# A two-layer diffusion backbone on one core: modulation units moved from the attention to the keys and values, output projection columns tied to residual adds, opening reordered

## The chip, the cores and the metric

The kernel runs on one core of a Trainium2 chip. Five engines work on their own instruction streams, each strictly in the order in which its instructions stand: PE (matrix products), DVE (vector), ACT (activations and copies), POOL and SP; SP issues the DMAs of this kernel. The metric is device time in microseconds (us); lower is better. Three runs of the kernel before took 1841.46, 1844.3 and 1845.71 us, median 1844.3.

## The reference

Two layers act on 512 latent tokens (x) and 256 context tokens (ctx) of width 1024. Layer 0 is windowed grouped-query attention with a sink, layer 1 is retention; each is followed by a SwiGLU FFN. In front of and behind each stands a modulation, whose six parts come from a product of the activated condition with `ada_w`:

```python
for i in range(DEPTH):
    mx = jnp.split(c_act @ ada_w[i] + ada_b[i], 6, axis=-1)
    mc = jnp.split(cc_act @ ada_w[i] + ada_b[i], 6, axis=-1)
    h_x = modulate(rms_norm(x, norm1_g[i]), mx[0], mx[1])
    h_c = modulate(rms_norm(y_ctx, norm1_g[i]), mc[0], mc[1])
    ...
    x = x + mx[2] * out_x
    x = x + mx[5] * swiglu(modulate(rms_norm(x, norm2_g[i]), mx[3], mx[4]), ffn_w_in[i], ffn_w_out[i])
    ...
```

Parts 0 and 1 are needed before the first key can be computed, part 2 at the residual add behind the attention, parts 3 and 4 at the first FFN, part 5 behind it.

## The kernel before

**Number format.** Weights and hidden tiles are split into a high and a low half: `whi` is a copy rounded on ACT (L137 or L162, 128x1024), `wlo` the difference on DVE (L138 or L163). A product is three matmuls: whi with the high hidden half, wlo with the high one, whi with the low one (`mm3`, L142; `keys` and `values` do the same with lines of their own, L392 and L403).

**The opening** (up to `St.close()`) loads x, the first two parts of `ada_w` as four quarters (`adaQ`, 4 x 512 KB each), the key and value weights, the context, rotary tables and masks, all issued by SP in program order. `stats0`, `ada_quarter`, `hidden0`, `keys` and `values` stand in a hand-written order for PE, DVE and ACT (`manual_schedule`). `ada_quarter(q)` makes the modulation of 2 of 8 hidden tiles: 32 products of 32 condition columns on PE (64 instructions), `rows` copied by ACT, two transposes on PE, then on DVE three small operations for the latent stream (s = 0) and three for the context (s = 1). `hidden0(s, k...)` then makes the scaled tile `hs` on DVE, the high half of `h` on ACT and the low half on DVE. `keys(s, q)` and `values(s, q)` use the hidden tiles 2q and 2q + 1. `split_w` splits the next of four key and value weights. The DMA tiles of quarters and of two of these weights share the tag `adan` with 8 buffers.

**The attention** follows: 24 blocks (4 head groups x 4 latent and 2 context blocks) whose instructions a scheduler interleaves. A block scores four heads on PE (L614), takes the minimum with mask and sink on DVE (L615), exponentials on ACT, the scaling on POOL (L628), transposes on PE (L637), copies, and value products on PE (L649). The query projections (`make_q`) of the next group stand between the blocks of the first three groups. After blocks 14, 16, 18 and 20 `ada_unit` makes four more pieces of modulation, units 4, 5 (part 2), 8 (part 4, tiles 0 to 3) and 6 (part 3, tiles 0 to 3): each loads four 512 KB tiles through the two `wraw` buffers that the weight stream uses, 32 products on PE (64 instructions, L286), a copy, one transpose (L291), two small DVE operations.

**The output projection** works on eight output tiles d in two batches of four weights: for each batch first the latent stream, then the context. Each tile is 24 matmuls into one of two `pj` banks, `gated_add` on DVE (L241) adds it to the residual and frees the bank, `add_square` collects the norm. The remaining columns of parts 3 and 4 (tiles 4 to 7 of each, eight in all) are made on DVE by `ada_tile` (L258, two instructions of 128x1024 a tile), one behind each of the first eight adds of the loop, and nothing but the scheduler sets where they stand on DVE.

## Time and profile before

The profiled execution took 1842.23 us, of which the span of its instructions is 1840.4 us.

| what | value |
|---|---|
| busy share of the span | PE 97%, weight loads 83%, DVE 61%, ACT 37%, POOL 7% |
| chain of work that ended last | PE 85%, DVE 6%, ACT 3%, DMA 2%, POOL 2% |
| granted TensorE clock, mean of the span | 0.995 |
| HBM read | 174.29 MB, 96 GB/s over the span |
| opening, up to the last value product | 0 to 83 us |
| attention | 85 to 326 us |
| output projection | 326 to 390 us |

Busy time of PE is the union of matmuls whose ends are modelled, so a busy PE may still be short of its peak rate: consecutive 128x512 matmuls start 0.23 us apart at full clock though each is listed with 0.39 us. A row of the timeline shows start, length, engine, line, operation, tiles and, in brackets, how long the engine sat idle before it and what released it.

### The profile page before, as it was taken

The numbers are of one execution on the slowest core, as the hardware profiler recorded it, in microseconds if no ns is written. First come the engines' busy times: TensorE is split into PE (matmuls) and PEld (weight loads), VectorE is DVE, ScalarE is ACT, GpSimd is POOL, SyncE is SP. The second block draws the span as 40 slices with busy tenths as digits, with TensorE's granted clock in tenths as the row PEclk, the third lists the DMA queues.
The fourth block names the chain that finished last, engine by engine and source line by source line (L and its number), as shares of the span: only waits on it lengthen the run. The fifth ranks groups of instructions, "written<-read, shape, count | busy, mean of one in ns | idle before, by whom it ended". The sixth has DMA issues, their size and how long they took to land.

```text
span 1840.4 us, 26468 instructions
## 1 busy us (share of the span) xinstructions
PE 1787.8 (97%) x10718; PEld 1534.0 (83%) x10718; DVE 1126.5 (61%) x2005; ACT 688.1 (37%) x1198; POOL 126.3 (7%) x228
## 2 busy tenths in 40 slices
PE   5999999999999999999999999999999989999999
PEld 4877766788888888888888888888888889999998
DVE  6787676768544545363675553553552698777774
ACT  5676666343221212121252322322421364445442
POOL 0044433000000000000011000010010000000000
PEclk9999999999999999999999999999999999999999
DMA  8100035535332425162521230220220333333232
GB/s 339 52 27 12 1 103 185 172 103 161 103 99 86 123 71 170 50 218 78 172 71 46 69 92 24 80 81 24 92 74 19 92 105 92 102 115 115 78 95 80
DMA packets 50955, 178.11 MB, mean 97 GB/s; under 512 B 5648, under 2 KB 6032, under 8 KB 50576
## 3 DMA queue, kind: packets, MB, share of 16 engines
q1 hardware_dynamic: 50832, 176.41, 30.6%
q8 instruction: 84, 1.38, 0.3%
q14 instruction: 39, 0.32, 0.1%
HBM read 174.29 MB, written 2.10 MB: 96 GB/s over the span
## 4 chain that ended last, share of the span: by engine, by line
PE 85%; DVE 6%; ACT 3%; DMA 2%; POOL 2%; issue 1%; SPq 0%; DVEq 0%; POOLq 0%; ACTq 0%
PE pj L146 10%; PE pj L145 10%; PE pj L147 10%; PE Y L811 6%; PE gu L145 4%; PE gu L146 4%; PE gu L147 4%; PE Z L811 3%; PE guc L147 2%; PE guc L145 2%; PE guc L146 2%; PE pv L145 2%; PE pv L147 2%; PE pv L146 2%; PE pv L1032 2%; PE pv L1033 2%
## 5 line engine op out<-in xcount | busy, mean ns | idle before, releaser
L137 ACT CAST whi<-wraw 128x1024 fp32r<-128x1024 f32 x174 | 182.3, 1049 | 261.1 <-PE pj L147 147.0
L138 DVE TENSOR_TENSOR wlo<-wraw,whi 128x1024 fp32r<-128x1024 f32 x174 | 215.4, 1239 | 82.1 <-ACT whi L137 81.1
L146 PE MATMUL pj<-h,wlo 128*128 128x512 f32 (+1 forms) x512 | 181.9, 355 | 4.4 <-DVE wlo L138 4.3
L145 PE MATMUL pj<-h,whi 128*128 128x512 f32 (+1 forms) x512 | 184.2, 360 | 1.7 <-DVE res L241 1.0
L147 PE MATMUL pj<-h,whi 128*128 128x512 f32 (+1 forms) x512 | 180.5, 354 | 0.2 <-DVE h L231 0.2
L241 DVE SCALAR_TENSOR_TENSOR res<-pj,mod,res 128x512 f32<-128x512 f32 (+1 forms) x160 | 104.7, 656 | 113.3 <-PE pj L147 112.8
L258 DVE CUSTOM_DVE_ANT_0 junk<-adaw,crow_sb,small_sb 128x1024 bf16<-128x1024 f32 x96 | 123.1, 1282 | 36.8 <-DMA adaw<-in_adaT_dram 34.4
L145 PE MATMUL pj<-ax,whi 128*128 128x512 f32 x352 | 138.3, 393 | 0.0
L146 PE MATMUL pj<-ax,wlo 128*128 128x512 f32 x352 | 137.5, 391 | 0.0
L145 PE MATMUL gu<-h,whi 128*128 128x512 f32 x352 | 137.4, 390 | 0.0
L146 PE MATMUL gu<-h,wlo 128*128 128x512 f32 x352 | 137.3, 390 | 0.0
L147 PE MATMUL pj<-ax,whi 128*128 128x512 f32 x352 | 137.1, 389 | 0.0
L147 PE MATMUL gu<-h,whi 128*128 128x512 f32 x352 | 136.9, 389 | 0.0
L146 PEld LDWEIGHTS pj<-h,wlo 128*128 128x128 f32 x512 | 97.6, 191 | 17.1 <-DVE wlo L138 5.3
L145 PEld LDWEIGHTS pj<-h,whi 128*128 128x128 f32 x512 | 97.4, 190 | 16.0 <-issue 1.5
L147 PEld LDWEIGHTS pj<-h,whi 128*128 128x128 f32 x512 | 97.4, 190 | 13.4 <-issue 0.8
L147 PE MATMUL guc<-h,whi 128*128 128x256 f32 x352 | 99.7, 283 | 0.0
L146 PE MATMUL guc<-h,wlo 128*128 128x256 f32 x352 | 99.6, 283 | 0.0
L145 PE MATMUL guc<-h,whi 128*128 128x256 f32 x352 | 99.6, 283 | 0.0
L162 ACT CAST whi<-wraw 128x1024 fp32r<-128x1024 f32 x59 | 61.7, 1053 | 76.9 <-PE pj L147 34.9
L106 ACT ACTIVATE hn<-gu 128x512 f32<-128x512 f32 x22 | 13.2, 598 | 197.4 <-PE gu L147 197.4
L163 DVE TENSOR_TENSOR res<-pv,res 128x512 fp32r<-128x512 f32 x24 | 16.6, 692 | 114.0 <-ACT res L162 114.0
(307 smaller groups left out, 4361.3 us busy)
## 6 DMA issues: line engine op xcount, KB each, us to landing
wraw<-in_wst_dram SPq DMA_DIRECT2D x214, 512.0 KB, 3.6
adaw<-in_adaT_dram SPq DMA_DIRECT2D x64, 512.0 KB, 4.2
adan<-in_adaQ_dram SPq DMA_DIRECT2D x16, 512.0 KB, 7.7
wraw<-in_adaN_dram SPq DMA_DIRECT2D x16, 512.0 KB, 4.3
res<-in_xT_dram SPq DMA_DIRECT2D x16, 256.0 KB, 5.2
res<-in_cT_dram SPq DMA_DIRECT2D x8, 256.0 KB, 6.3
crow_sb<-in_crow_dram SPq DMA_DIRECT2D x2, 1024.0 KB, 5.1
out_dram<-res SPq DMA_DIRECT2D x8, 256.0 KB, 2.0
```

Source lines behind the costliest of these rows:

```text
L137: nc.scalar.copy(hi, raw)
L138: nc.vector.tensor_tensor(lo, raw, hi, op=sub)
L145: nc.tensor.matmul(o, whi, xhi, start=first, stop=False)
L146: nc.tensor.matmul(o, wlo, xhi, start=False, stop=False)
L147: return nc.tensor.matmul(o, whi, xlo, start=False, stop=last)
L162: nc.scalar.copy(hi, t)
L163: return nc.vector.tensor_tensor(lo, t, hi, op=sub)
L241: nc.vector.scalar_tensor_tensor(res[d], o, mods[l, s][:, part, d:d + 1], res[d], mult, add)
L258: after(nc.vector.tensor_tensor_reduce(junk, w, cr[:, s * 1024:(s + 1) * 1024], 1.0, sm_t[:, C_ADAB + l * 48 + j:C_ADAB + l * 48 + j + 1], ...
L811: nc.tensor.matmul(o, p, r, start=first and k + i == 0, stop=k == 3 and i == 2, skip_group_check=not first)
L1032: nc.tensor.matmul(vo, hi[:, tok], wk_[1][:, cs], start=False, stop=False)
L1033: nc.tensor.matmul(vo, lo[:, tok], wk_[0][:, cs], start=False, stop=k == KT - 1)
```

## The change

The four units leave the attention. Their 16 loads are issued by SP right behind the masks, through the 8 `adan` buffers, after the load of the first query weight (`q0_raw`), which is issued early too; every later weight load stands behind them on SP. Their products, copies and transposes are written into the opening's manual order, between `keys` and `values`; the fourth one's transpose stands behind `values(0, 2)`.

In the opening, work is put between the products of a quarter and its transposes (`fill`): two dummy matmuls (`busy`, whose result is overwritten) in quarter 0, halves of `values` or `keys` in the others. Only the three DVE operations of the latent stream stand ahead of its hidden tiles; those of the context are handed back as a function (`c1`) and come later. The low half of a weight (`split_low`) is separated from the high half (`split_w`), and the fourth weight's high half is made earlier. `keys` runs each of its three products over both hidden tiles before the next. The first `values(0, 2)` matmul is held behind the last `keys` matmul.

In the output projection `WO_ADA` names the adds that an `ada_tile` follows: (0, 0) to (0, 6) and (1, 2), that is five in the first batch and three in the second; each now must stand behind its add on DVE (an order without a semaphore).

```diff
-UNITS_AT = (14, 16, 18, 20)
 UNITS = (4, 5, 8, 6)
+WO_ADA = [(0, d) for d in range(7)] + [(1, 2)]
...
+    def unit_load(u):
+        w = []
+        for kk in range(4):
+            w.append(T(st_p, 1024, "adan", 8))
+            nc.sync.dma_start(w[kk], adaN[u, kk])
+        return w
+
+    def ada_unit(u, w):
         part, d0 = u // 2, u % 2 * 4
-        o = pj()[:, 0:P]
+        o = pT()[:, 0:P]
         for kk in range(4):
-            w = T(rp, 1024, "wraw", 2)
-            nc.sync.dma_start(w, adaN[u, kk])
...
         rows = T(cp, 256, "rows", 2)[:, 0:P]
         nc.scalar.copy(rows, o)
+        def finish():
...
+        return finish
...
-    def ada_quarter(q, w):
+    def ada_quarter(q, w, fill):
...
         nc.scalar.copy(rows, o)
+        fill()
         t = pT()[:, 0:256]
...
+        columns(0)
+        return lambda: columns(1)
...
+    q0_raw = w_raw()
+    wu = [unit_load(u) for u in UNITS]
...
+    def busy(n):
+        nc.tensor.matmul(kvv[2][:, :n], ones, res0[0][0][:, :n], start=True, stop=True)
...
         stats0(0)
         split_w(st_p)
-        ada_quarter(0, wq[0])
-        hidden0(0, 0, 1)
+        c1 = ada_quarter(0, wq[0], lambda: busy(256))
+        busy(SX)
+        hidden0(0, 0, 1, between=(split_low,))
+        c1()
         split_w(st_p)
+        split_low()
         keys(0, 0)
         split_w(rp)
+        split_low()
         squares0(1)
-        ada_quarter(1, wq[1])
+        c1 = ada_quarter(1, wq[1], lambda: values(0, 0, (0, 1)))
         hidden0(0, 2, 3)
-        values(0, 0)
+        c1()
+        values(0, 0, (2, 3))
         rms(1, bank=pT)
         keys(0, 1)
-        ada_quarter(2, wq[2])
+        c1 = ada_quarter(2, wq[2], lambda: values(0, 1, (0, 1)))
+        c1()
         hidden0(1, 0, 1)
+        split_w(rp)
         hidden0(1, 2, 3)
         hidden0(0, 4, 5)
-        split_w(rp)
-        values(0, 1)
-        ada_quarter(3, wq[3])
+        values(0, 1, (2, 3))
+        c1 = ada_quarter(3, wq[3], lambda: keys(1, 0))
+        c1()
+        split_low()
         hidden0(1, 4, 5)
-        keys(1, 0)
         keys(1, 1)
         hidden0(0, 6, 7)
+        c1 = ada_unit(UNITS[0], wu[0])
         keys(0, 2)
         hidden0(1, 6, 7)
+        c1()
+        c1 = ada_unit(UNITS[1], wu[1])
         values(1, 0)
         values(1, 1)
+        c1()
...
+        c1 = ada_unit(UNITS[2], wu[2])
         keys(1, 2)
+        c1()
         keys(0, 3)
-        keys(1, 3)
+        last_key = keys(1, 3)
+        c1 = ada_unit(UNITS[3], wu[3])
...
-        values(0, 2)
+        after(values(0, 2), [last_key])
+        c1()
...
-            if 6 * g + i in UNITS_AT:
-                ada_unit(UNITS[UNITS_AT.index(6 * g + i)])
...
-                gated_add(s, 0, 2, d, o, res)
+                ins = gated_add(s, 0, 2, d, o, res)
                 add_square(s, d, res[d])
-                if ada_wo and (s or d < 4):
-                    ada_tile(0, *ada_wo.pop(0), (0, 1), cr, wo_p, 4)
+                if (s, d) in WO_ADA:
+                    ada_tile(0, *ada_wo.pop(0), (0, 1), cr, wo_p, 4, [ins])
```

More of the change, by code (lines that the diff above doesn't have):

```diff
@@ L131, in w_parts, with next_w @@
         return T(pool, 1024, "whi", bufs, F32R), T(pool, 1024, "wlo", bufs, F32R)
-    def next_w(pool, own=2):
-        raw = w_raw()
+    def next_w(pool, own=2, raw=None):
+        raw = raw or w_raw()
         hi, lo = w_parts(pool, own)
@@ L240, in gated_add @@
     def gated_add(s, l, part, d, o, res):
-        nc.vector.scalar_tensor_tensor(res[d], o, mods[l, s][:, part, d:d + 1], res[d], mult, add)
+        return nc.vector.scalar_tensor_tensor(res[d], o, mods[l, s][:, part, d:d + 1], res[d], mult, add)
     def cond_rows(pool):
@@ L272, in dit_kernel @@
     ln_exp_turn()
-    def ada_unit(u):
+    def unit_load(u):
[5 more added lines that the diff above has]
+    def ada_unit(u, w):
         part, d0 = u // 2, u % 2 * 4
-        o = pj()[:, 0:P]
+        o = pT()[:, 0:P]
         for kk in range(4):
-            w = T(rp, 1024, "wraw", 2)
-            nc.sync.dma_start(w, adaN[u, kk])
             for a in range(2):
@@ L285, in ada_unit @@
                     c0 = a * 512 + j * P
-                    nc.tensor.matmul(o[32 * j:32 * j + 32, :], ccol[:, 2 * kk + a, :], w[:, c0:c0 + P],
+                    nc.tensor.matmul(o[32 * j:32 * j + 32, :], ccol[:, 2 * kk + a, :], w[kk][:, c0:c0 + P],
                                      start=kk + a == 0, stop=kk + a == 4)
@@ L289, in ada_unit @@
         nc.scalar.copy(rows, o)
-        t = pj()[:, 0:P]
-        nc.tensor.transpose(t, rows, ident)
-        tv = t.rearrange("p (j c) -> p c j", c=32)
-        for s in range(2):
-            nc.vector.tensor_tensor(mods[0, s][:, part, d0:d0 + 4], tv[:, s, :],
-                                    sm_t[:, C_ADAB + 4 * u:C_ADAB + 4 * u + 4], op=add)
+        def finish():
+            t = pT()[:, 0:P]
+            nc.tensor.transpose(t, rows, ident)
+            tv = t.rearrange("p (j c) -> p c j", c=32)
+            for s in range(2):
+                nc.vector.tensor_tensor(mods[0, s][:, part, d0:d0 + 4], tv[:, s, :],
+                                        sm_t[:, C_ADAB + 4 * u:C_ADAB + 4 * u + 4], op=add)
+        return finish
     def ada_quarter_load(q):
@@ L320, in ada_quarter, with columns @@
         bias = sm_t[:, C_ADAB:C_ADAB + 16].rearrange("p (f d) -> p f d", f=2)[:, :, 2 * q:2 * q + 2]
-        for s in range(2):
+        def columns(s):
             col = mods[0, s][:, 0:2, 2 * q:2 * q + 2]
@@ L341, in split_w, with split_low @@
     def split_w(pool):
-        w = raw[len(wkv)]
         wkv.append((T(pool, 1024, "whi", 2, F32R), T(pool, 1024, "wlo", 2, F32R)))
-        split(w, *wkv[-1])
+        nc.scalar.copy(wkv[-1][0], raw[len(wkv) - 1])
+    def split_low():
+        i = lows.pop(0)
+        nc.vector.tensor_tensor(wkv[i][1], raw[i], wkv[i][0], op=sub)
+    lows = [0, 1, 2, 3]
     wkv = []
@@ L373, in stats0, with hidden0 @@
         rms(s, bank=pT)
-    def hidden0(s, *ks):
+    def hidden0(s, *ks, between=()):
         y, ts = ssq[s], []
@@ L381, in hidden0 @@
             nc.scalar.activation(h[s][k][0], ts[-1], AF.Identity, bias=mods[0, s][:, 0, k:k + 1])
+        for b in between:
+            b()
         for k, t in zip(ks, ts):
@@ L387, in keys, with values @@
             o = kvx[j] if s == 0 else kvc[:, j * SC:(j + 1) * SC]
-            for k in (2 * q, 2 * q + 1):
-                ws = slice(k * P, (k + 1) * P)
-                (whi, wlo), (xhi, xlo) = wkv[j], h[s][k]
-                for i, (a, b) in enumerate(((whi, xhi), (wlo, xhi), (whi, xlo))):
-                    nc.tensor.matmul(o, a[:, ws], b, start=k + i == 0 and (s == 0 or j == 0),
-                                     stop=k == KT - 1 and i == 2, skip_group_check=s == 1)
-    def values(s, q):
-        for t in ((0, 1, 2, 3), (4, 5))[s]:
+            for i, (a, b) in enumerate(((0, 0), (1, 0), (0, 1))):
+                for k in (2 * q, 2 * q + 1):
+                    last = nc.tensor.matmul(o, wkv[j][a][:, k * P:(k + 1) * P], h[s][k][b],
+                                            start=k + i == 0 and (s == 0 or j == 0),
+                                            stop=k == KT - 1 and i == 2, skip_group_check=s == 1)
+        return last
+    def values(s, q, tiles=None):
+        first = None
+        for t in tiles or ((0, 1, 2, 3), (4, 5))[s]:
             tok = slice((t - 4 * s) * P, (t - 4 * s) * P + P)
@@ L402, in values @@
                 for i, (a, b) in enumerate(((hi, whi), (hi, wlo), (lo, whi))):
-                    nc.tensor.matmul(o, a[:, tok], b[:, cs], start=k + i == 0 and t % 2 == 0,
-                                     stop=k == KT - 1 and i == 2, skip_group_check=True)
+                    ins = nc.tensor.matmul(o, a[:, tok], b[:, cs], start=k + i == 0 and t % 2 == 0,
+                                           stop=k == KT - 1 and i == 2, skip_group_check=True)
+                    first = first or ins
+        return first
     with tc.manual_schedule(engines={mybir.EngineType.PE, mybir.EngineType.DVE, mybir.EngineType.Activation}):
@@ L478, in dit_kernel, with make_q @@
     q, stats = {}, {}
-    def make_q(j):
-        w = next_w(ap, 1)
+    def make_q(j, raw=None):
+        w = next_w(ap, 1, raw)
         qs = T(ap, 36, "qs", 4).rearrange("p (f n) -> p f n", f=3)
@@ L547, in dit_kernel @@
     wsel[0] = 2
-    q0 = make_q(0)
+    q0 = make_q(0, q0_raw)
     with tc.manual_schedule(engines={mybir.EngineType.PE}):
-        values(0, 2)
+        after(values(0, 2), [last_key])
+        c1()
         rope_key(kn[0])
```

## The prediction

> **What bounds the kernel now.** I read the chain of waits first, then windows of the three touched stages, then the timeline where PE waits.

> ```profile
> PE 85%; DVE 6%; ACT 3%; DMA 2%; POOL 2%; issue 1%; SPq 0%; DVEq 0%; POOLq 0%; ACTq 0%
> ```

> PE sets the end: what shortens PE's list or a wait on it counts, work elsewhere only where PE waits for it. The windows give PE, weight loads, DVE, ACT and POOL busy, the granted clock, DMA share and GB/s:

> ```profile
> 10.00:20.00 10.00, 6.05 (x68) 3.61 (x68) 7.90 (x27) 5.10 (x8) 0.00 (x0) 1.00 1.03 420
> ...
> 18.77:22.18 3.41, 0.44 (x2) 0.20 (x2) 3.27 (x9) 1.01 (x2) 0.00 (x0) 1.00 1.02 419
> 22.18:25.60 3.42, 3.28 (x8) 2.47 (x9) 3.12 (x4) 2.63 (x4) 0.00 (x0) 0.50 1.03 407
> 42.66:46.07 3.41, 1.60 (x60) 1.33 (x52) 3.10 (x7) 2.00 (x4) 0.00 (x0) 1.00 1.01 354
> ...
> 353.27:356.69 3.42, 0.90 (x4) 0.30 (x2) 3.42 (x7) 0.42 (x1) 0.00 (x0) 1.00 0.00 0
> 356.69:360.10 3.41, 1.65 (x4) 1.36 (x5) 3.41 (x6) 0.00 (x0) 0.00 (x0) 0.50 0.24 29
> ```

> The early opening is short of DMA and DVE, not of PE. 420 GB/s makes 1.25 us for each 512 KB tile. After a 3.4 us stretch with PE 0.44 or 0.90 us busy, the clock was 0.50 in the next; after 1.60 us it was not.

> ```profile
> 46.27 1.03 ACT L162 CAST whi<-adan 128x1024 fp32r<-128x1024 f32 x1
> 47.21 0.36 ACT L315 COPY rows<-pT 128x256 f32<-128x256 f32 x1
> ...
> 47.35 0.39 PE L403 MATMUL kvv<-whi,h 128*128 128x256 f32 x1 [3.09 <-ACT whi L162]
> 47.62 0.44 PE L318 MATMUL pT<-const_sb,rows 128*128 128x128 f32 x2
> ```

> The first matmul of values(0, 2) had slipped ahead of the last quarter's transposes and held PE 3.09 us; but the `rows` copy which these need ended at 47.57 anyway.

> ```profile
> 355.97 1.28 DVE L258 CUSTOM_DVE_ANT_0 junk<-adaw,crow_sb,small_sb 128x1024 bf16<-128x1024 f32 x1
> 357.17 1.22 DVE L138 TENSOR_TENSOR wlo<-wraw,whi 128x1024 fp32r<-128x1024 f32 x1
> ...
> 354.66 0.47 PE L145 MATMUL pj<-h,whi 128*128 128x512 f32 x1 [0.96 <-DVE res L241]
> 358.45 0.79 PE L146 MATMUL pj<-h,wlo 128*128 128x512 f32 x1 [3.31 <-DVE wlo L138]
> ```

> In the output projection DVE works through modulation columns, so the second batch's first low half is late: PE waits 0.96 and 3.31 us, then starts about a dozen matmuls 0.43 us apart instead of 0.23.

> **Part 1, the opening: +7.9 us.** A unit is 64 PE instructions; 64 of the same shape took 1.95 us at 42.31 (L312). Four, with four transposes of some 0.05 to 0.2 us, make 8.0 us. What the new order gives back I walked step by step from the rows of before.
> - *Quarter 0.* Dropping three of the six DVE column operations (19.83 to 20.77) brings the hidden tiles 0.5 us forward; but both low weight halves (1.23 us each) now stand behind them on DVE, and keys(0, 0) needs them: it ends near 27.0 instead of 26.8. The dummy matmuls (about 0.45 and 0.9 us) fill an idle stretch; they save the eight slow matmuls (0.2 each), but keys(0, 0) then waits for DVE instead. Taken: 0; bounds -1.6 (all eight) and +0.9 (dummies in the way).
> - *Quarter 1.* Half of values(0, 0) runs in the 1.46 us that PE waited for `rows`; keys(0, 1) still waits for its hidden tiles, whose DVE start at 31.6 does not move (seven context squares stand ahead). It ends near 36.3 instead of 36.55.
> - *Quarter 2.* The fill is 12 matmuls 0.12 apart, 1.45 us, but `rows` was ready at 39.02: the transposes move from 39.07 to about 39.45, and DVE's chain (columns, context, tiles 4 and 5) 0.4 us later with them.
> - *Quarter 3.* PE loses the 3.09 us wait, but `rows` still stands on ACT behind the high halves of tiles 4 and 5, ready about 47.25. keys(1, 0), 1.45 us, is done in the wait. Together PE is 1.9 us ahead at 47.6.
> - *The units' weights.* Behind the masks (44.96 in before, near 44.5 now) land the query weight and 16 tiles, 1.25 us apart: the units are complete at 50.9, 55.8, 60.7 and 65.6. PE is there at 49.1, 54.5, 59.4 and 67.0: the first costs 0.5 us of waiting, the others nearly nothing, since tiles are used as they land. The second unit's last tile takes the fourth weight's buffer, freed by its low half at 49.9, in time. Each reuse of the eight buffers also waits for PE, 4 to 9 us before PE needs the tile.
> - *Behind.* values(0, 2) ends at 71.9 instead of 64.78. ACT reaches the key copies only after the fourth unit's `rows` (68.8), the query's high half stands behind six of them (3.4 us), its low half behind the rotary steps on DVE: 74.9, where it was 67.0. That wait, 1.02 us in before, comes back whole.
> Later weight loads stand behind the 16 on SP; the next lands near 66.9 and is needed near 89. So 74.9 - 67.0 = +7.9. Bounds: +1 (all waits named above, 3.1 + 1.5 + 0.7 + 1.6 us, are gone) and +12 (two half-clock stretches of 1.7 us and DMA 1 us late at two units).

> **Part 2, the attention: -10.8 us.** The 256 unit matmuls (L286) are 12.9 us of busy PE there, more than 8.0, as each run of a few is cut into by scores. Are they additive, or do they fill gaps? Blocks 6 to 11 ended 55.2 us after block 5, with 16.6 us of query projection (two tiles of 24 matmuls 0.228 us apart and 24 matmuls 0.118 apart) and 2.4 of norms: 36.2 for the blocks. Blocks 18 to 23 took 48.4 with 6.4 of units and 5.8 of output projection: 36.2 again. So filler adds. But with the units gone, blocks 19 to 21 stand almost bare in the new PE order, and PE waited 0.5 to 0.7 us several times there for DVE, POOL and ACT; I give back 2.1 us. Bounds: -4 (only the waits for unit tiles and switching) and -13.8.

> **Part 3, the output projection: -3.9 us.** Five columns instead of eight in the first batch free 3 x 2.9 us of DVE (two of 1.28 and their accumulator reads each) ahead of the second batch's low halves. The first is then done near 351, before PE asks. Gone: 0.96 + 3.31 us and 12 x 0.2 us of half clock, with the pauses between, 7.1 us. The three later tiles cost nothing: DVE needs 2.9 + 0.75 + 0.69 = 4.3 us beside 5.5 us of PE per output tile; without that cover each would cost 2.9. But the scheduler now puts 23 more of its matmuls (5.2 us) into the attention; the first batch, DVE-bound until 350 (DVE 9.8 of 10 busy from 335 to 355), takes only about 2 us of that, the rest becomes a wait for banks: +3.2. Bounds: -7.1 and -1.

> [...]

> **Sum.** +7.9 - 10.8 - 3.9 = -6.8 us on the profiled execution, 1842.23 us (span 1840.4): 1835.4. That run lies 2.07 below the median 1844.3, so the forecast is 1837.5; its own range, from half of each part's bounds, 1832 to 1842.

> **Rivals.**
> - *The opening gains what its waits show* (3.1, 1.5, 0.7 and the slow matmuls, 6.9 in all): for it, these rows are idle PE; against it, ACT and DVE end the next wait each time. 1837.5 - 6.9 = 1830.6.
> - *Units were cover in the attention*: for it, blocks 18 to 23 hold many short waits for DVE and POOL; against it, the equal 36.2. -4 in place of -10.8, but then the early output matmuls cost nothing either (-3.2): 1841.
> - *Slower: the unit loads are late.* The eight tiles of the last two units reuse buffers that PE frees. If they come at the pace of the attention's unit loads, 4.3 us from issue to landing, one after the other, the last lands at 55.8 + 8 x 4.3 = 90 instead of 65.6, and PE, in order, stands 23 us at 67: 1860. For it: SP waits in order for each buffer. Against it: four buffers come free at once. It decides from about 3 us a tile (55.8 + 8 x 3.1 - 67 = 14 us, twice the forecast's gain).
> - *The tie does nothing*: the low halves stay behind the columns. Against it: in the new DVE order the first stands behind the add of (1, 1), ahead of four column instructions. Without part 3: 1841.4.

> **Chances.** A difference of 0.2% (3.7 us) is about what runs of this kernel can tell. Forecast 0.54, opening gains 0.13, cover 0.15, slower 0.13, tie 0.05. Faster by over 0.2% (below 1840.6): 0.13, the forecast's own lower part 0.48, a share of the middle cases 0.09: 0.70. Within: 0.16. Slower: 0.14. The range 1828 to 1847 leaves out the late loads and little else.

> **What would show it.** The opening: values(0, 2) ending near 72 us, the first query product near 75, unit waits below 1 us. The attention: no unit line, last value product near 326. The output projection: no wait over 1 us for a low half, no 0.50 clock there. Wrong if PE waits several us for unit tiles, or blocks 18 to 23 take over 45 us.

## The result and the profile after

| | median | runs | ratio to the kernel before |
|---|---|---|---|
| before | 1844.54 us | 4 (1841.46 to 1845.71) | |
| after | 1832.42 us | 4 (1831.61 to 1833.5) | 0.9937, 95% interval 0.992 to 0.9954 |

The profiled execution of the changed kernel took 1832.84 us, its span 1831.05. The forecast was 1837.5; the time lies 5.1 below it, near the lower end of the range of 1832 to 1842.

The chain of waits of the changed kernel has the same owner as before:

```profile
PE 86%; DVE 5%; ACT 2%; DMA 2%; POOL 2%; issue 1%; SPq 0%; POOLq 0%; ACTq 0%; DVEq 0%
```

So the time can be counted along PE. I cut both spans at three PE instructions: the second product of the first query (the first that needs its low half), the attention's last value product, and the first product of the FFN.

| stretch of the span | before | after | difference |
|---|---|---|---|
| opening, to the query's second product | 67.04 | 76.95 | +9.91 |
| attention, to its last value product | 258.18 | 248.14 | -10.04 |
| output projection, to the first FFN product | 70.02 | 62.71 | -7.31 |
| rest | 1445.2 | 1443.25 | -1.95 |

23 more matmuls of the output projection stand ahead of the last value product than before, 0.228 us each, 5.2 us in all. For like work (these 23 counted in the same stretch both times) the attention gave 15.3 us and the output projection 2.1.

Not all of these stretches repeat equally well from profile to profile. The opening of the changed kernel stands unchanged in five profiles, its own included, and took 75.62 to 77.27 us in them; the opening of before took 67.04 and 68.67 us in two. So a difference of up to 1.65 us there can be chance. The attention repeats within 0.1 us where the clock is the same: 248.1 to 248.2 us in three profiles with full clock in it.

The opening, in the timeline of the changed kernel (start, length, engine, line, operation, tiles, idle time before it and its releaser):

```profile
46.19 1.38 ACT L406 ACTIVATE h<-hs,mod 128x512 fp32r<-128x512 f32 x2 [1.21 <-DVE hs L405]
47.48 0.35 ACT L324 COPY rows<-pT 128x256 f32<-128x256 f32 x1
...
47.89 0.44 PE L328 MATMUL pT<-const_sb,rows 128*128 128x128 f32 x2 [2.21 <-ACT rows L324]
51.39 0.64 PE L291 MATMUL pT<-adan,ccol 128*32 128x128 f32 x16 [0.58 <-DMA adan<-in_adaN_dram]
52.62 0.65 PE L291 MATMUL pT<-adan,ccol 128*32 128x128 f32 x16 [0.58 <-DMA adan<-in_adaN_dram]
...
75.69 0.49 PE L145 MATMUL pj<-h,whi 128*128 128x512 f32 x1 [0.54 <-ACT whi L137]
76.95 0.50 PE L146 MATMUL pj<-h,wlo 128*128 128x512 f32 x1 [0.76 <-DVE wlo L138]
```

The last quarter's transposes still wait for `rows`, which ACT makes only behind the high halves of tiles 4 and 5. The 3.09 us stall of a slipped value product is replaced by this one of 2.21. The first unit waits twice for its tiles; the other three run through in 1.88 us each, from one start to the next. Both halves of the query's weight are waited for.

The waits of PE inside the attention (what waited, for what, us in total, times, longest); the first fence is before, the second after:

```profile
PE pT L637 <- POOL pr L628: 5.4, 10, 1.1
PE S L614 <- DVE stat L615: 2.2, 4, 0.7
PE pT L637 <- ACT tt L639: 1.5, 3, 0.7
PE pj L286 <- DMA wraw<-in_adaN_dram: 1.0, 3, 0.4
```

```profile
PE pT L682 <- POOL pr L673: 8.2, 14, 1.1
PE pT L682 <- ACT tt L684: 1.3, 4, 0.4
```

All rows of this view add up to 11.9 us before and 12.6 after. Two kinds have to be taken out for a comparison: the wait for the query's low half, which ends where the stretch begins (1.0 and 0.8), and the units' own tiles (1.0 before). What is left, PE's waits for POOL, DVE and ACT, is 9.9 us before and 11.8 after.

The same stretch by groups of six blocks, each cut at the end of its last value product (PE's waits of 0.15 us and more, in us; unit matmuls in the group; "more" are query and output products that the group holds after and not before; the first group's waits hold the query's):

| blocks | before | waits | unit matmuls | after | waits | more | difference for like work |
|---|---|---|---|---|---|---|---|
| 0 to 5 | 90.4 | 2.7 | 0 | 90.3 | 2.4 | 0 | 0.0 |
| 6 to 11 | 55.3 | 2.3 | 0 | 55.6 | 2.4 | 4 | -0.6 |
| 12 to 17 | 64.6 | 5.1 | 134 | 55.9 | 3.7 | 9 | -10.7 |
| 18 to 23 | 48.4 | 1.8 | 122 | 46.7 | 4.0 | 9 | -3.7 |

The units' instructions, with their transposes and from start to start, took 7.0 us of blocks 12 to 17 and 5.8 us of blocks 18 to 23. So in the one group their leaving gave more than they took, in the other less.

The output projection, in the timeline of the changed kernel, is:

```profile
325.66 1.05 ACT L137 CAST whi<-wraw 128x1024 fp32r<-128x1024 f32 x1
326.76 0.50 PE L145 MATMUL pj<-h,whi 128*128 128x512 f32 x1 [1.30 <-ACT whi L137]
...
327.88 0.80 PE L145 MATMUL pj<-h,whi 128*128 128x512 f32 x1 [0.61 <-ACT whi L137]
...
349.43 1.22 DVE L138 TENSOR_TENSOR wlo<-wraw,whi 128x1024 fp32r<-128x1024 f32 x1
```

The second batch's first low half, at 357.17 before, is at 349.43 and nobody waits for it. In its place PE waits right behind the attention, for the high halves of the third and fourth weight; and the granted clock is 0.51 and 0.50 there, as the windows of the changed kernel show (us, then PE, weight loads, DVE, ACT and POOL busy, granted clock, DMA share, GB/s):

```profile
20.00:23.40 3.40, 1.90 (x5) 0.58 (x4) 3.29 (x7) 2.03 (x3) 0.00 (x0) 0.99 1.01 413
23.40:26.80 3.40, 3.40 (x8) 1.86 (x8) 3.33 (x7) 1.81 (x4) 0.00 (x0) 0.50 1.06 418
...
323.70:327.10 3.40, 1.42 (x9) 0.76 (x9) 1.81 (x4) 2.23 (x6) 0.00 (x0) 1.00 0.14 39
327.10:330.50 3.40, 2.79 (x7) 2.16 (x7) 2.26 (x3) 1.14 (x2) 0.00 (x0) 0.51 1.00 390
```

The half clock behind the second batch's wait is gone; one of 6.8 us, two such windows long, has come in at 327.1. The opening keeps a half-clock stretch in this profile (0.50 from 23.40), the dummy matmuls notwithstanding.

### The profile page after: what moved, and what is told of

It is laid out like the page before. It is cut to its first block, busy times and chain, and to the rows that moved or that the text cites. A ratio compares the mean times of both kernels' runs of the same rounds, so it can differ in the third digit from the quotient of the medians.

```text
span 1831.1 us, 26491 instructions
## 1 busy us (share of the span) xinstructions
PE 1781.6 (97%) x10722; PEld 1531.3 (84%) x10722; DVE 1126.8 (62%) x2005; ACT 686.3 (37%) x1198; POOL 126.2 (7%) x228
## 4 chain that ended last, share of the span: by engine, by line
PE 86%; DVE 5%; ACT 2%; DMA 2%; POOL 2%; issue 1%; SPq 0%; POOLq 0%; ACTq 0%; DVEq 0%
PE pj L145 10%; PE pj L146 10%; PE pj L147 10%; PE Y L854 6%; PE gu L146 4%; PE gu L145 4%; PE gu L147 4%; PE Z L854 3%; PE guc L147 2%; PE guc L145 2%; PE guc L146 2%; PE pv L145 2%; PE pv L147 2%; PE pT L682 2%; PE pv L146 2%; PE pv L1075 2%
## 5 line engine op out<-in xcount | busy, mean ns | idle before, releaser
L138 DVE TENSOR_TENSOR wlo<-wraw,whi 128x1024 fp32r<-128x1024 f32 x174 | 215.1, 1237 | 81.9 <-ACT whi L137 81.0
L145 PE MATMUL pj<-h,whi 128*128 128x512 f32 (+1 forms) x512 | 184.7, 361 | 3.1 <-ACT whi L137 2.5
L146 PE MATMUL pj<-h,wlo 128*128 128x512 f32 (+1 forms) x512 | 181.3, 354 | 0.8 <-DVE wlo L138 0.8
L241 DVE SCALAR_TENSOR_TENSOR res<-pj,mod,res 128x512 f32<-128x512 f32 (+1 forms) x160 | 104.6, 655 | 110.7 <-PE pj L147 110.0
L258 DVE CUSTOM_DVE_ANT_0 junk<-adaw,crow_sb,small_sb 128x1024 bf16<-128x1024 f32 x96 | 123.0, 1281 | 39.2 <-DMA adaw<-in_adaT_dram 34.8
L145 PE MATMUL pj<-ax,whi 128*128 128x512 f32 x352 | 138.3, 393 | 0.0
L146 PE MATMUL pj<-ax,wlo 128*128 128x512 f32 x352 | 137.5, 390 | 0.0
L145 PE MATMUL gu<-h,whi 128*128 128x512 f32 x352 | 137.4, 390 | 0.0
L146 PE MATMUL gu<-h,wlo 128*128 128x512 f32 x352 | 137.3, 390 | 0.0
L145 PEld LDWEIGHTS pj<-h,whi 128*128 128x128 f32 x512 | 97.6, 191 | 18.3 <-ACT whi L137 4.0
L146 PEld LDWEIGHTS pj<-h,wlo 128*128 128x128 f32 x512 | 97.7, 191 | 12.6 <-DVE wlo L138 1.1
L146 PE MATMUL guc<-h,wlo 128*128 128x256 f32 x352 | 99.6, 283 | 0.0
L145 PE MATMUL guc<-h,whi 128*128 128x256 f32 x352 | 99.6, 283 | 0.0
L162 ACT CAST whi<-wraw 128x1024 fp32r<-128x1024 f32 x57 | 59.6, 1052 | 76.5 <-PE pj L147 37.1
L163 DVE TENSOR_TENSOR res<-pv,res 128x512 fp32r<-128x512 f32 x24 | 16.6, 691 | 112.5 <-ACT res L162 112.5
```

Source lines behind the costliest of these rows:

```text
L138: nc.vector.tensor_tensor(lo, raw, hi, op=sub)
L145: nc.tensor.matmul(o, whi, xhi, start=first, stop=False)
L146: nc.tensor.matmul(o, wlo, xhi, start=False, stop=False)
L162: nc.scalar.copy(hi, t)
L163: return nc.vector.tensor_tensor(lo, t, hi, op=sub)
L241: return nc.vector.scalar_tensor_tensor(res[d], o, mods[l, s][:, part, d:d + 1], res[d], mult, add)
```

## The experiments

All of them compute the whole reference. "Opening", "attention", "output" and "rest" are the stretches of the table above.

**Three parts undone, one at a time.** The columns without their tie, as before, in the changed kernel:

```diff
-                if (s, d) in WO_ADA:
-                    ada_tile(0, *ada_wo.pop(0), (0, 1), cr, wo_p, 4, [ins])
+                if ada_wo and (s or d < 4):
+                    ada_tile(0, *ada_wo.pop(0), (0, 1), cr, wo_p, 4)
```

> The changed kernel with the eight modulation columns of the output projection placed as before (behind the first eight adds, no order on DVE); all else as changed. If the placing makes the gain there (our theory), DVE works through all eight columns ahead of the second batch's low halves again: a wait of 3 us or more of PE for a low half returns, the stretch from the last value product of the attention to the first FFN product grows from 62.7 us (changed kernel) to 68 to 71 us, and the time rises by 5 to 8 us. If the placing does nothing, the stretch stays within 1 us and the time within 2 us of the changed kernel.

Measured: 1841.42 us (12 runs), ratio 0.9989 (0.998 to 0.9998). The timeline of this kernel has the old wait again, the low half behind a row of column instructions with only adds between them:

```profile
357.64 1.28 DVE L258 CUSTOM_DVE_ANT_0 junk<-adaw,crow_sb,small_sb 128x1024 bf16<-128x1024 f32 x1
358.85 1.22 DVE L138 TENSOR_TENSOR wlo<-wraw,whi 128x1024 fp32r<-128x1024 f32 x1
360.12 0.80 PE L146 MATMUL pj<-h,wlo 128*128 128x512 f32 x1 [3.31 <-DVE wlo L138]
```

Output took 69.02 us instead of 62.71. The time rose by 9.0 us, where 5 to 8 were expected: its profile has two half-clock stretches, at 237.0 and 984.5, that the changed kernel's has not. Without the tie the rest of the change is worth 0.1%: the opening and the attention nearly cancel.

The units back in the attention, with the new opening order kept (`unit_load` and the four `ada_unit` calls out of the opening, the old `ada_unit` at `UNITS_AT`):

```diff
-    wu = [unit_load(u) for u in UNITS]
...
-        c1 = ada_unit(UNITS[0], wu[0])
...
+            if 6 * g + i in UNITS_AT:
+                ada_unit(UNITS[UNITS_AT.index(6 * g + i)])
```

> The changed kernel with the four units back behind attention blocks 14, 16, 18 and 20, loaded through the two weight buffers as before; new opening order and new placing of the columns kept. If the units cost more in the attention than in the opening (our theory), the last product that uses the first query's low half comes about 8 us earlier than in the changed kernel, the attention from there to its last value product grows by about 15 us less the 5.2 us of output projection that it no longer takes in, and the time rises by 2 to 7 us. If the units only fill gaps in the attention, the time falls by 5 us or more.

Measured: 1835.59 us, 0.9956 (0.9944 to 0.9968), 3.2 slower than the changed kernel. Opening 64.98: the four units cost it 76.95 - 64.98 = 11.97 us, not the 8.0 that their instructions take, and the new order by itself gives 67.04 - 64.98 = 2.06, both to within the 1.65 us above. Attention 261.40, 13.3 more than after, of which two half-clock stretches (at 223.5 and 267.9) are at most 3.4, half of their length; with the 5.2 us of early matmuls that it no longer takes in, 15.1 for like work, or 18.5 with those stretches counted.

The old opening order, with the units in it (quarters without fill, both halves of a weight split together, `keys` looping over tiles first):

> The changed kernel with the opening's order as before (no dummy matmuls, transposes right behind their products, both halves of a weight split together, context columns at once, key products tile by tile), but the units kept in the opening at the same places and the first value product of the third block still held behind the last key product. If the reordering is worth little because ACT and DVE end the next wait (our theory), PE's second product of the first query moves by less than 2.5 us and the time by less than 2.5 us. If the named waits were real gains, both rise by 5 to 7 us.

Measured: 1833.24 us, 0.9946 (0.9934 to 0.9958): 0.8 above the changed kernel, opening 77.69 instead of 76.95. With units in the opening the new order is worth 0.7 us by these two profiles, which is less than the spread of the opening, so no gain is shown. Output took 59.86 here with the same two waits behind the attention, but no half clock there: that clock cost the changed kernel 2.85 us. The kernel with the units behind the keys, below, is another such case (59.88).

**One part alone**: only the tie, put into the kernel before.

```diff
-                if ada_wo and (s or d < 4):
-                    ada_tile(0, *ada_wo.pop(0), (0, 1), cr, wo_p, 4)
+                if (s, d) in WO_ADA:
+                    ada_tile(0, *ada_wo.pop(0), (0, 1), cr, wo_p, 4, [ins])
```

> The kernel before with nothing changed but the placing of the eight modulation columns in the output projection. If DVE's columns made the wait of 3.3 us (our theory), that wait and the half clock behind it are gone: the stretch from the attention's last value product to the first FFN product falls from 70.0 to about 63 us, the time by 5 to 7 us. If other work makes the low halves late, less than 2 us.

Measured: 1837.74 us, 0.9966 (0.9953 to 0.9979), 6.0 below the kernel before. Output 62.82, from 70.02: -7.2, where the prediction had 7.1. The third weight's high half is made right behind the attention here too (at 329.30, 0.6 us behind the last value product), but PE still has 23 matmuls more of the first two tiles to do, and doesn't wait for it.

**The dummy matmuls left out** (`lambda: None` for the fill of quarter 0, and no `busy(SX)`).

> The changed kernel without the two dummy matmuls of the first quarter. If they only fill idle time (our theory: keys(0, 0) ends when DVE has its low halves, not when PE is fast), PE's second product of the first query stays within 0.8 us of 76.95 us and the time within 1.5 us of the changed kernel. If they keep the clock up to any use, that moment comes 1.5 us or more later; if they are in the way, 1 us or more earlier.

Measured: 1833.11 us, 0.9942 (0.993 to 0.9955). The query's second product starts at 76.87 instead of 76.95, although the half clock lasted 6.8 us instead of 3.4 in this opening (from 21.1): PE waits for the first hidden tile from ACT there either way (2.19 us without the dummies, 1.33 with them), and the next quarter's products begin at 27.46 and 27.54. The dummies are worth nothing that can be measured. The clock of the opening does differ: all four profiles without them have half clock there, beginning between 20.5 and 23.1 us (22.18 before, 21.1 here), and five of the eight with them have none; whether the dummies make that difference is not shown. Of the five profiles with the same opening, those without half clock took 75.62, 76.43 and 77.27 us, those with it 75.82 and 76.95.

**The third output weight prepared early.** The third pair of halves gets a pool `op` of its own, which outlives the attention and is shared with the query weights; before, its memory was covered by the attention's pool until that closed.

```diff
+    op = A.enter_context(tc.tile_pool(name="op", bufs=1, reuse_waits="tile"))
...
-        w = next_w(ap, 1, raw)
+        w = next_w(op, 1, raw)
...
-        w = [next_w(wo_p) for _ in range(4)]
+        w = [next_w((op, wo_p)) for _ in range(4)]
```

> The changed kernel with the split halves of the output projection's third weight (and those of every third query weight) in a buffer of their own that the attention's memory does not cover. In the changed kernel PE stands 1.55 and 0.87 us behind the attention's last value product for that weight's high half, which ACT starts at the moment the attention ends, and the clock is 0.50 for 6.8 us behind it. If the memory is the cause (our theory), both waits are gone and no 0.50 clock follows at that place; the stretch from the last value product to the first FFN product falls from 62.7 to 58 to 60.5 us, the rest of the 5.8 us being held by DVE's columns. If ACT is late for another reason, nothing moves by over 1 us.

Measured: 1828.53 us, 0.9917 (0.9904 to 0.9931), 3.9 below the changed kernel. Both waits behind the attention are gone, and the half clock at 327. Yet output is only 0.7 us shorter (61.98, where 58 to 60.5 was expected), since a new wait stands a little later in its timeline (lines are shifted by 3 here):

```profile
342.71 1.27 DVE L261 CUSTOM_DVE_ANT_0 junk<-adaw,crow_sb,small_sb 128x1024 bf16<-128x1024 f32 x1
342.94 0.47 PE L148 MATMUL pj<-h,whi 128*128 128x512 f32 x1 [1.51 <-DVE res L244]
344.25 2.35 DVE L141 TENSOR_TENSOR wlo<-wraw,whi 128x1024 fp32r<-128x1024 f32 x2
345.52 0.51 PE L149 MATMUL pj<-h,wlo 128*128 128x512 f32 x1 [2.11 <-DVE wlo L141]
```

PE arrives earlier, and now the five columns of the first batch hold back both an add that frees a bank and the second batch's low halves; behind that wait comes a half-clock stretch, 3.4 us from 345.9. The attention is 5.0 us shorter (243.14), with six more early matmuls in it: PE's waits for POOL fall from 8.2 us to 4.8 there. That the output matmuls which fill PE are ready sooner is the likely reason, but not shown by itself.

**The columns spread further**, on top of the early third weight: four in each batch.

```diff
-WO_ADA = [(0, d) for d in range(7)] + [(1, 2)]
+WO_ADA = [(0, 1), (0, 3), (1, 1), (1, 3)] + [(0, d) for d in range(4, 8)]
```

> As e6_third_weight_early, and the modulation columns follow the adds (0, 1), (0, 3), (1, 1), (1, 3), (0, 4), (0, 5), (0, 6), (0, 7): one fewer in the first batch, spread out. If DVE is what holds the first batch once the third weight is early (our theory), the stretch from the last value product to the first FFN product falls by another 1 to 3 us; if PE is, nothing changes within 0.5 us; if the last column is now late for the FFN's scale, it grows.

Measured: **1823.22 us** (1822.51 to 1823.63), ratio **0.9886** (0.9871 to 0.9902), the fastest of this study, 9.2 below the changed kernel. Output 56.45, 5.5 us shorter (1 to 3 expected), without a wait of PE from 310 to 365 us that is longer than 0.45.

**The columns spread further, alone**: the same line in the changed kernel, the third weight left where it was.

> The changed kernel with the columns tied two to the first batch's latent adds (0, 1) and (0, 3), two to its context adds, and four to the second batch, but the third output weight left where it was. Theory (the third weight's high half, late after the attention, is the first limit, and PE's waits and half clock there give DVE the time that the columns need): the two waits after the attention stay, 1.5 and 0.9 us, no other wait goes, and the time stays within 1 us of the changed kernel, 1831.4 to 1833.4. Rival (DVE's columns alone set the first batch): the 5.3 us that separated the kernel with the early third weight from the one with later columns as well come here too, some 1827.

Measured: 1832.94 us, 0.9951 (0.9938 to 0.9965). Output 62.62, as in the changed kernel, and its timeline has that kernel's first wait unchanged:

```profile
325.46 0.80 PE L145 MATMUL pj<-h,whi 128*128 128x512 f32 x1 [1.30 <-ACT whi L137]
```

So the two limits stand one behind the other. While PE loses 5 us to the late third weight and the half clock, DVE has time for either order of the columns; only when the first is gone does the second decide, for 5.3 us.

**The units behind the keys**: the first three units one step later each in the opening's order (the fourth stays where it was), and tiles 4 and 5 behind the last quarter's columns, so that `rows` is not behind them on ACT.

```diff
-        hidden0(0, 4, 5)
         values(0, 1, (2, 3))
         c1 = ada_quarter(3, wq[3], lambda: keys(1, 0))
         c1()
+        hidden0(0, 4, 5)
...
-        c1 = ada_unit(UNITS[0], wu[0])
         keys(0, 2)
         hidden0(1, 6, 7)
-        c1()
...
+        c1 = ada_unit(UNITS[0], wu[0])
         values(1, 1)
         c1()
```

> The changed kernel with two moves in the opening: the hidden tiles 4 and 5 of the latent stream behind the fourth quarter's columns, so that ACT copies that quarter's rows before their high halves, and each unit one product group later (first one behind values(1, 0)). If PE waits there for ACT's order (2.37 us) and for the first unit's loads (0.75 us twice), as our theory has it, both waits go and PE's second product of the first query comes 2.5 to 4 us earlier than 76.95 us, the time 2 to 4 us lower. If DVE or the loads set the pace anyway, less than 1 us.

Measured: 1833.63 us, 0.9939 (0.9926 to 0.9951): a miss. The wait for `rows` is gone, but its time comes back (timeline of PE in this kernel):

```profile
48.20 0.50 PE L417 MATMUL pj<-h,whi 128*128 128x512 f32 x1 [1.09 <-ACT h L406]
...
63.59 0.64 PE L291 MATMUL pT<-adan,ccol 128*32 128x128 f32 x16 [0.70 <-DMA adan<-in_adaN_dram]
```

PE now waits for the hidden tiles and for the third unit's weights instead. The query's second product starts at 76.45, half a microsecond earlier, which is inside the spread of the opening. The opening is paced by what feeds PE: the units cost 12.0 us in the changed kernel, 11.5 here (against the same 64.98, whose order has tiles 4 and 5 at the other place) and 10.65 in the old order (77.69 against 67.04). Between these three the spread allows no choice, but all are more than the 8.0 of their instructions.

**The units in the attention of the fastest kernel** (that kernel, with the units placed as in the second experiment).

> The fastest kernel so far (1823.22 us) with the units back in the attention. Theory (the units cost 12.0 us in the opening and at least 13.3 in the attention, whatever the output projection does): 3 us slower than that kernel, as the changed kernel with units in the attention was 3.2 slower than the changed one: about 1826.3, attention stretch 12 to 15 us longer. Rival (once the output projection takes early matmuls without loss, the units are cover in the attention that these matmuls no longer give): not slower, 1820 to 1823.5.

Measured: 1833.9 us, 0.9947 (0.9935 to 0.996): 10.7 slower than the fastest kernel, where 3 was expected. The sign held, the size didn't. Its opening is 10.25 us shorter (65.57), its attention 17.5 longer (260.81), its output 6.1 longer. The last is just the 27 matmuls that no longer run early (27 x 0.228 = 6.2): PE waits no longer there. In the attention, 12.8 are the units' own instructions and at most 3.4 two half-clock stretches (at 224.2 and 268.6); and PE's waits in this stretch add up to 13.3 us with the units, 2.0 of them for the units' own tiles, and 7.8 without. Less the 6.2 of early matmuls, that is 15.5 of the 17.5. The profiled execution (1836.18) lies 2.3 above its median, so that its stretches add up to more than 10.7. The early third weight does little for this attention, it seems because the units take the places that the output matmuls would fill: 411 query and output products of 128x512 or 128x256 stand ahead of its last value product, 438 in the fastest kernel.

## Why the prediction was right, and where not

The time came out faster, and the three parts had the signs forecast, each with another size: +9.9 for +7.9, -15.3 for -10.8, -2.1 for -3.9, all for like work. That is -7.4 on the touched stretches, where the forecast had -6.8. That these two lie so close is luck: the parts were off by +2.0, -4.5 and +1.8, which cancel. The rest of the span gave 1.95 more, and the profiled executions lie differently to their medians (before 2.3 below, after 0.4 above), which adds 2.7: together the 12.1 between the medians.

- **The opening.** The steps were right in kind: `rows` stayed behind ACT, the dummies were worth nothing (without them 76.87), only the first unit waited, the query's halves came back as a wait. The size was 2.0 us short: the last quarter's transposes ended so that the first unit began at 49.69 instead of 49.1, and that unit waited 1.6 us instead of 0.5. These two make 1.7 of the 2.0. (On the mean of the five like openings and of the two before, 76.4 and 67.9, the cost is 8.6 and the shortfall 0.7, so how far the term was off in general stays open.) The term that was mis-sized is thus "the first costs 0.5 us of waiting": its four tiles were taken to be there by 50.9, and PE's waits for the last two ended at 51.39 and 52.62; the masks ahead of them landed at 45.22 instead of 44.5.
- **The attention.** The correction, "I give back 2.1 us" for blocks that stand almost bare, was right in kind and size: PE's waits in blocks 18 to 23 rose from 1.8 to 4.0 us, and that group gave 3.7 us for units of 5.8. The term that was mis-sized is the price, "12.9 us of busy PE" for all units. Blocks 12 to 17 gave 10.7 us for units of 7.0. Of the 3.7 us above that, 1.4 are waits that went with the units, 0.8 of them for their own tiles; the other 2.3 lie between matmuls without a wait of 0.15 us. PE changed over to unit matmuls 23 times in the attention, and from the start of a score to the start of a unit matmul behind it 0.27 us passed (median of 11), from score to score 0.12. That these changes make all of the 2.3 is not shown. The warning was in the profile of before: the prediction's check of additivity read blocks 6 to 11 and 18 to 23, 36.2 us of block each, and not blocks 12 to 17, whose 64.6 us leave 39.2 by the same count (16.6 of query projection, 2.4 of norms, 6.4 of units).
- **The output projection.** The mechanism was right, and its size: alone, the tie gave 7.2 (7.1 forecast). The early matmuls' loss was forecast at 3.2 and came out at 5.1 (7.2 by the tie alone, 2.1 for like work in the changed kernel). The reason given for it, a first batch bound by DVE, was not what stood first. The late third weight was (1.55 + 0.87 us beyond the matmuls' own spacing, and 2.85 of half clock, 5.3 in all); DVE's columns came next, as the kernel with the early weight shows. "No 0.50 clock there" was wrong: it moved from 356.7 to 327.1.
- **The rest**, 1.95 us, was not foreseen, and the change doesn't touch it. PE has the same 2.28 us from one matmul's start to the next in the second layer's retention in both profiles, at 981.3 and 973.9, with PE 1.61 and 1.62 of 3.40 us busy in the window from there; the next window had a clock of 0.51 before and 1.00 after. That stretch may make some 1.6 us of it, an estimate from what one such stretch took in the attention (last section).
- **The rivals.** Late unit loads: PE waited for unit tiles only in the first unit, 0.75 us twice from start to start. Cover in the attention: true of blocks 18 to 23 by 2.2 us, but refuted as a whole, since the attention gave 15.3 and not 4, and the units' return to the fastest kernel made it slower by 10.7. The tie doing nothing: refuted by the tie alone and by its removal. The opening that gains all its waits: no, the new order gave 2.1 without units and 0.7 with them, of 6.9, the second within the spread.

## What to carry to other kernels

Price filler on an engine that works in order by its spacing from start to start, add what changing over to it costs (here 0.27 us from a score to a unit matmul against 0.12 from score to score), and take off the waits that it covered. Compare the sums of waits rather than single ones, and do it for every group of like blocks: here one group gave 10.7 us for 7.0 of filler and the next 3.7 for 5.8. When work is pulled ahead of a boundary, ask what its last input needs to exist: a buffer whose memory is freed at the boundary was the next wait here (1.55 and 0.87 us), and a second limit behind it shows only once the first is gone. A move that costs in one stretch and pays in another by nearly the same amount (here 12.0 against 15) is worth what it lets other work do in the place that it leaves: 3 us in the changed kernel, 10.7 in the fastest one.

## What the runs showed of the hardware that was not expected

The same piece of the program, with the same gap in PE's work, was followed by half clock in one profile and by full clock in another. The profiles before and after have it at these places (same columns as above):

```profile
981.30:984.70 3.40, 1.61 (x7) 1.11 (x7) 3.40 (x4) 1.43 (x2) 0.55 (x1) 1.00 0.12 10
984.70:988.10 3.40, 3.40 (x10) 2.65 (x9) 0.58 (x1) 0.00 (x0) 0.00 (x0) 0.51 0.75 242
```

```profile
973.90:977.30 3.40, 1.62 (x7) 1.12 (x7) 3.40 (x4) 1.41 (x2) 0.54 (x1) 1.00 0.10 10
972.19:975.60 3.41, 2.21 (x9) 1.30 (x7) 2.54 (x5) 2.09 (x3) 2.25 (x2) 1.00 0.00 0
975.60:979.01 3.41, 2.83 (x12) 2.16 (x13) 2.26 (x3) 0.00 (x0) 0.00 (x0) 1.00 0.49 145
```

Counted in these two profiles, each cut like this from 14 us on, and only where the window itself is at full clock: the seven windows followed by half clock had PE 0.44, 0.90, 1.44, 1.47, 1.63, 1.67 and 1.91 us busy. Of the other windows, 17 had PE less than 2.4 us busy, the least 1.60, and 1030 had it busy for longer; all were followed by full clock. Half clock lasted 3.4 us in five of the seven cases and 6.8 us in two, from 356.69 before and from 327.15 in the changed kernel. The same part of the program met half clock in some profiles and not in others: the attention of the changed kernel had full clock throughout, that of the kernel with the old tie a half-clock stretch at 237.0 us. One stretch came with 1.6 us in the attention: the same attention took 248.1 to 248.2 us in three profiles without one and 249.7 to 249.8 in three with one. Runs of one kernel spread by more (1841.45 to 1847.28 in 17 runs of the kernel before); how much of that is the clock no run here shows.
